# Loads of rotated queries and keys: 32 rows outermost, four parts within

## The chip, the cores and the metric

The program runs on one core of a Trainium2 chip. The metric is the device time of one execution in microseconds (us). The kernel before is given by the median of three runs, and by one further execution that the hardware profiler recorded.

## What is computed

One transformer block on 1024 tokens of width 1024, in float32: a feed-forward block, a token mixer, a second feed-forward block, and a norm. The change lies in the mixer, which has two attentions. Cut to what matters:

```python
# first attention: 8 heads, each with two score maps c = 0, 1 over 64 dimensions
q = apply_rope(q, cos, sin); k = apply_rope(k, cos, sin)
s = einsum('bqhcd,bkhcd->bhcqk', q, k) * HEAD_DIM ** -0.5      # causal
p = softmax(s); a = p[:, :, 0] - lam * p[:, :, 1]
o = einsum('bhqk,bkhe->bqhe', a, v)                            # then a norm per head
# second attention: 16 heads in 2 groups; compressed, selected-block and window branches
qr = apply_rope(q, cos, sin); ks = apply_rope(k_slc, cos, sin); kw = apply_rope(k_win, cos, sin)
o = g0 * o_cmp + g1 * o_slc + g2 * o_win
# mixer
merged = sigmoid(g_a) * (y_da @ w_proj_da) + sigmoid(g_b) * (y_ns @ w_proj_nsa)
x = x + merged @ w_out
```

A rotation pairs dimension d with d + 32, so a head's 64 dimensions are two halves of 32.

## The kernel before, in words

**Layout.** Tokens lie along the free dimension, features on the 128 partitions. Float32 matrices are multiplied as a high and a low part, three products each (`mm3`, lines 52 to 54: `whi`, `wlo` are a weight block's parts). The probabilities and values of the attentions are split into two fp16 halves (`th`, `tl`, lines 974 to 999).

**Rotated queries and keys go through DRAM.** `rope_pair` (from line 612) projects two column blocks of 128, which hold the two halves (32 dimensions each) of four heads or score maps, rotates them on VectorE (lines 625 and 626 read the product out of its bank) and GpSimd, splits them into `rh` and `rl`, and stores those (line 635) into a scratch tensor with dimensions

```python
K.s_q = [dr.tile([3, 2, 4, 32, T], F32, name=f"sq{p}") for p in range(4)]   # part, half, slot, row, token
K.s_k = [dr.tile([2, 2, 4, 32, T], F32, name=f"sk{p}") for p in range(4)]
```

The stores take the 128 rows (slot, row) outermost. The loads read back one slot: `h` (two parts, high and low) and `a` (two halves) give four parts of 32 rows each, which fill 128 partitions. Two neighbouring rows of a part lie 4 KiB apart, two parts 512 KiB. For queries, two such tiles are loaded (`z` = 0: high, low; `z` = 1: low, high), so that two matrix products of 128 rows give the full score.

| Load | Line | Count | Bytes of one, one contiguous run |
|---|---|---|---|
| first attention, queries, `qt<-sq` | 938 | 128 | 128 KB, 1 KB |
| first attention, keys, `kt<-sk` | 1036 | 16 | 512 KB, 4 KB |
| second attention, keys, `kt<-skv` | 1063 | 4 | 512 KB, 4 KB |
| second attention, queries, `qt<-sqn` | 1088 | 64 | 256 KB, 2 KB |

**Who consumes them.** `scores` (line 919) multiplies queries by keys into a PSUM tile `S`; VectorE adds the mask and takes the row's extreme (line 926); ScalarE takes the exponential (line 928); GpSimd and VectorE scale and combine the two maps (lines 960, 962); TensorE transposes blocks of 128 (line 974), ScalarE and VectorE split them into halves (977, 978), and TensorE multiplies them by the values (997 to 999). At the end of half a head the output is squared and summed (lines 1005, 1007, 1014).

**What else runs there.** Between these steps `Filler` deals out projections that do not depend on the attention: queries, keys and values of later heads, gates, and the output projection. They take one PSUM bank (`gm`). Their weight blocks of 512 KB come into `wst` (two buffers, line 1216, before that line 143) and are split by ScalarE and VectorE (lines 1226 and 85, and 89 for the blocks before).

**What sets the order.** The order on each engine is fixed when the program is built. All DMAs are issued by SyncE, one after another in that order; each waits there for what it must follow (a store for its data, a load for its buffer or for the store that it reads). ScalarE and VectorE also work strictly in their order, so a split of weights that waits for its block holds what stands behind it, the exponentials among it. `rh` and `rl` have one buffer each: a new one waits until the stores of the last have landed. The first attention runs from about 970 us to 1460 us of the span, with two heads' projections ahead of it.

Of the kernel before, what the change touches and what calls it, by code (L numbers as in the profile page):

```python
# [7 lines left out]
F32 = mybir.dt.float32  # L8
# [922 lines left out]
def da_queries(K, h, m):  # L931
    nc = K.nc
    qt = []
    p, s0 = h // 2, (h % 2) * 2
    for c in range(2):
        t = K.qp.tile([P, 2, 2 * P], F32R, tag="q", name="qt")
        for z in range(2):
            nc.sync.dma_start(out=t[:, z].bitcast(F32),
                              in_=K.s_q[p][z:z + 2, :, s0 + c, :, m * 256:(m + 1) * 256].rearrange("h a d t -> (h a) d t"))
        qt.append(t)  # L940
    return qt

# [84 lines left out]
def da_load(K, h):  # L1027
    drain([da_load_keys(K, h)])


def da_load_keys(K, h):
    p, s0 = h // 2, (h % 2) * 2
    K.k = []
    for c in range(2):
        t = K.kp.tile([P, T], F32R, tag="k", name="kt")
        K.nc.sync.dma_start(out=t.bitcast(F32), in_=K.s_k[p][:, :, s0 + c].rearrange("h a d t -> (h a) d t"))
        K.k.append(t)
        yield

# [19 lines left out]
def ns_load_key(K, i):  # L1059
    g, br = i // 2, i % 2  # L1060
    pool, tag = [(K.rope, "cR"), (K.rope, "sR"), (K.mp, "m13"), (K.mp, "rh")][i]
    t = pool.tile([P, T], F32R, tag=tag, name="kt")
    order_after(K, K.nc.sync.dma_start(out=t.bitcast(F32), in_=K.s_kv[:, :, br * 2 + g].rearrange("h a d t -> (h a) d t")),
                K.last)
    K.nk[g, br] = t

# [17 lines left out]
def ns_queries(K, hd, H):  # L1084
    qt = []
    for z in range(2):
        t = K.qp[hd % 2].tile([P, TB], F32R, tag=f"q{z}", name="qt")
        K.nc.sync.dma_start(out=t.bitcast(F32), in_=K.s_qns[hd // 4][z:z + 2, :, hd % 4, :, H * TB:(H + 1) * TB]
                            .rearrange("h a d t -> (h a) d t"))
        qt.append(t)  # L1090
    return qt

# [89 lines left out]
def order_after(K, inst, first):  # L1182
    if first is not None:
        K.tc.add_manual_dep(inst.ins, first.ins.name,
                            mybir.DependencyInfo(mybir.DependencyClass.NoSync, mybir.DependencyReason.DATA),
                            reason="order the filler's weights")
# [207 lines left out]
def da_phase(K, cg):  # L1394
    nc = K.nc
    with ExitStack() as ctx:
# [3 lines left out]
        for n, f in enumerate(da_units(K, 0)[:2] + da_units(K, 1)):  # L1400
            if n == 2:
                da_load(K, 0)
            if n == 3:
                da_load_values(K, 0)
            if n == 4:
                q0 = da_queries(K, 0, 0)
                da_split_values(K, 0, K.gm, "gm")
            drain([f()])
# [28 lines left out]
        for p in range(4):  # L1437
            fill.pace(3 * (p + 1) if p < 2 else 6 + ng * (p - 1), PACE_DA)
            for h in (2 * p, 2 * p + 1):
                if h:  # L1440
                    da_load(K, h)
                if h in (4, 6):
                    da_load_values(K, h)
                for m in range(4):
                    qt = q0 if h + m == 0 else da_queries(K, h, m)
                    if h == 4:
                        ns_load_key(K, m)
                    if m == 2 and h + 1 in (1, 2, 3, 5, 7):
                        da_load_values(K, h + 1)
                    res = da_scores(K, h, m, qt, fill.step)  # L1450
                    if pend:
                        finish(*pend)
                    if m == 0 and h in (4, 6):
                        da_split_values(K, h, K.tr, "tr")
                    if m == 3 and h + 1 in (1, 2, 3, 5, 7):
                        da_split_values(K, h + 1, K.tr, "tr")
                    pend = (h, m, res)
            fill.end()
# [6 lines left out]
def ns_phase(K):  # L1465
    nc = K.nc
    K.low = LOW_NS
    with ExitStack() as ctx:
# [5 lines left out]

        K.qp, K.pcp = [pool("nq0")], [pool("npc0")]
        q0 = ns_queries(K, 0, 0)
        pc0 = ns_compressed(K, 0, 0)
        K.qp.append(pool("nq1"))
# [39 lines left out]
        for g in range(2):  # L1518
            for pr in range(4 * g, 4 * g + 4):
                for H in range(2):  # L1520
                    pc = ns_compressed(K, pr, H) if pr + H else pc0
                    y = K.op.tile([P, TB], F32, tag="y", name="y")
                    for par in range(2):
                        hd = pr * 2 + par
                        qt = ns_queries(K, hd, H) if hd + H else q0
                        for m in (2 * H, 2 * H + 1):
                            res = ns_scores(K, hd, m, qt, g, fill.step)
                            if pend:
                                finish(*pend)
                            pend = (hd, m, res, (pc, y), g, par)  # L1530
# [242 lines left out]
```

## Time and profile before

| | before |
|---|---|
| runs: median (lowest, highest) | 2915.92 us (2915.45, 2916.07) |
| profiled execution: its time, its span | 2920.45 us, 2918.7 us |
| TensorE busy | 2795.0 us (96%) |
| VectorE, ScalarE, GpSimd busy | 2001.1, 1392.5, 790.6 us |
| DMA moved, mean rate | 467.74 MB, 160 GB/s |
| share of the 16 DMA engines' span on SyncE's queue | 46.8% |

The profile is of one execution. A row of a timeline has the start in us from the span's start, the duration in us, the engine, the kernel's line, the operation, the tile written, an arrow, the tiles read, and a count where rows were merged; in brackets the time that the engine stood idle before it and what released it. PE is TensorE, DVE VectorE, ACT ScalarE, SPq SyncE's DMA queue; an SPq row's duration is that of issuing, not of the transfer. A row of a stretch has its bounds, its length, the busy time of TensorE, of its weight loads, VectorE, ScalarE and GpSimd with instruction counts in brackets, the granted clock of TensorE as a share of full speed, the mean busy share of the 16 DMA engines, and GB/s. A row of waits has who waited for what, the total in us, how many times, and the longest.

### The profile page before, as it was taken

Reading aid. Unit: us, or ns where it says so; the run is one execution under the profiler, and the core shown is the slowest. Engines: PE = TensorE matmul, PEld = TensorE weight load, DVE = VectorE, ACT = ScalarE, POOL = GpSimd, SP = SyncE. Lnnn points to the kernel's source line nnn. Section 1 sums busy time; section 2 is a strip of 40 time slices with the busy share of each in tenths; the row PEclk is TensorE's granted clock in tenths of the full one; section 3 lists DMA queues with packets and bytes.
Section 4 is the critical chain, followed back from the end, with each engine's and each line's share of the span. In section 5 each row is a group of like instructions: output and inputs, shape, how many; then the busy total and the mean of one; then the engine's idle time right before and its main releaser. Section 6 shows DMA issues by size and latency. Waiting matters only on the chain. (4 is left out here: it accounts for less than half of the span.)

```text
span 2918.7 us, 40265 instructions
## 1 busy us (share of the span) xinstructions
PE 2795.0 (96%) x14310; PEld 2038.4 (70%) x14310; DVE 2001.1 (69%) x3414; ACT 1392.5 (48%) x2391; POOL 790.6 (27%) x701
## 2 busy tenths in 40 slices
PE   8999999999999898989999999999999999999998
PEld 6644447887788776777778778888787854444886
DVE  7866866666588466767777777777443976675566
ACT  7533424442333244455566666777433653333443
POOL 3133321000044222322233333333242414223001
PEclk9999999999999999999999999999999999999999
DMA  4355548654456544444332226222843246444854
GB/s 163 120 201 180 174 170 276 217 185 141 137 188 227 192 144 135 167 143 136 131 121 91 84 86 202 88 87 81 305 153 122 80 143 222 158 173 165 296 181 145
DMA packets 208682, 467.74 MB, mean 160 GB/s; under 512 B 20448, under 2 KB 39136, under 8 KB 208480
## 3 DMA queue, kind: packets, MB, share of 16 engines
q1 hardware_dynamic: 208480, 465.16, 46.8%
q8 instruction: 113, 1.85, 0.3%
q14 instruction: 89, 0.73, 0.1%
HBM read 308.32 MB, written 156.76 MB: 159 GB/s over the span
## 5 line engine op out<-in xcount | busy, mean ns | idle before, releaser
L405 PEld LDWEIGHTS <-w 128*128 128x128 f16 x3024 | 297.7, 99 | 385.2 <-issue 35.6
L52 PE MATMUL gm<-hi,whi 128*128 128x512 f32 x880 | 352.9, 401 | 11.6 <-DVE m L626 7.5
L54 PE MATMUL gm<-hi,wlo 128*128 128x512 f32 x880 | 348.2, 397 | 1.4 <-DVE wlo L85 1.4
L53 PE MATMUL gm<-lo,whi 128*128 128x512 f32 x880 | 348.5, 396 | 0.0
L405 PE MATMUL Y<-tf,w 128*128 128x512 f16 x1296 | 298.4, 385 | 21.3 <-DVE u L443 17.1
L919 PE MATMUL S<-kt,qt 128*128 128x320 f32 (+5 forms) x1152 | 271.4, 357 | 17.5 <-ACT Pt L928 7.5
L85 DVE TENSOR_TENSOR wlo<-st,whi 128x1024 fp32r<-128x1024 f32 x154 | 197.4, 1300 | 114.9 <-ACT whi L89 114.0
L978 DVE TENSOR_TENSOR tl<-tr,th 128x512 f16<-128x512 f32 (+2 forms) x384 | 233.8, 618 | 57.2 <-ACT th L977 56.0
L977 ACT ACTIVATE th<-tr 128x512 f16<-128x512 f32 (+2 forms) x384 | 202.4, 542 | 142.1 <-PE tr L974 125.7
L926 DVE CUSTOM_DVE_ANT_0 S<-S,slab 128x896 f32<-128x896 f32 (+7 forms) x320 | 223.9, 709 | 64.4 <-PE S L919 58.6
L89 ACT ACTIVATE whi<-st 128x1024 fp32r<-128x1024 f32 x154 | 160.7, 1057 | 179.4 <-PE acc L54 109.4
L53 PE MATMUL acc<-wlo,whi 128*128 128x512 f32 (+1 forms) x628 | 244.1, 389 | 1.0 <-DVE wlo L85 1.0
L54 PE MATMUL acc<-whi,wlo 128*128 128x512 f32 (+1 forms) x628 | 242.8, 389 | 0.0
L52 PE MATMUL acc<-whi 128*128 128x512 f32 (+1 forms) x628 | 240.4, 387 | 0.0
L919 PEld LDWEIGHTS S<-kt,qt 128*128 128x128 f32 x1152 | 186.2, 195 | 35.1 <-ACT Pt L928 9.8
L1114 POOL TENSOR_SCALAR Ps<-Ps,l 128x384 f32<-128x384 f32 (+7 forms) x128 | 101.9, 796 | 377.9 <-DVE l L1112 279.3
L52 PEld LDWEIGHTS gm<-hi,whi 128*128 128x128 f32 x880 | 167.4, 190 | 45.1 <-DVE m L626 10.0
L405 PE MATMUL X<-h,w 128*128 128x512 f16 x864 | 195.3, 379 | 1.0 <-ACT s L415 1.0
L54 PEld LDWEIGHTS gm<-hi,wlo 128*128 128x128 f32 x880 | 166.9, 190 | 37.0 <-DVE wlo L85 2.0
L53 PEld LDWEIGHTS gm<-lo,whi 128*128 128x128 f32 x880 | 167.4, 190 | 30.6 <-issue 0.4
L85 DVE TENSOR_TENSOR wlo<-wst,whi 128x1024 fp32r<-128x1024 f32 x103 | 141.9, 1380 | 62.5 <-ACT whi L89 40.4
L521 POOL TENSOR_TENSOR u<-u,u 128x512 f32<-128x512 f32 x36 | 52.7, 1463 | 349.1 <-DVE sa L102 164.3
(340 smaller groups left out, 6063.2 us busy)
## 6 DMA issues: line engine op xcount, KB each, us to landing
wst<-in_win_dram SPq DMA_DIRECT2D x55, 512.0 KB
sw<-w2s SPq DMA_DIRECT2D x44, 512.0 KB
st<-sw SPq DMA_DIRECT2D x88, 256.0 KB
st<-saT SPq DMA_DIRECT2D x88, 256.0 KB
a<-in_f1w_dram SPq DMA_DIRECT2D x36, 512.0 KB
a<-in_f2w_dram SPq DMA_DIRECT2D x36, 512.0 KB
st<-saB SPq DMA_DIRECT2D x66, 256.0 KB
qt<-sq SPq DMA_DIRECT2D x128, 128.0 KB
```

What stands on the lines that cost most here:

```text
L52: first = nc.tensor.matmul(out, lhsT=w[0][:, wk], rhs=x[0], start=start, stop=False, skip_group_check=skip)
L53: nc.tensor.matmul(out, lhsT=w[0][:, wk], rhs=x[1], start=False, stop=False, skip_group_check=skip)
L54: nc.tensor.matmul(out, lhsT=w[1][:, wk], rhs=x[0], start=False, stop=stop, skip_group_check=skip)
L85: return nc.vector.tensor_tensor(out=lo, in0=src, in1=hi.bitcast(F32), op=ALU.subtract)
L89: nc.scalar.activation(out=hi, in_=src, func=AF.Copy)
L405: K.mark = nc.tensor.matmul(o, lhsT=w[:, a, m * h + k], rhs=x[k][:, b], start=start and k == 0 and i == 0, stop=k == h - 1 and i == 2, ski ...
L521: nc.gpsimd.tensor_tensor(out=a, in0=a, in1=b, op=ALU.mult)
L919: K.last = nc.tensor.matmul(S[:, o:o + n], lhsT=q, rhs=k[:, k0 + c:k0 + c + n], start=i == 0, stop=i == 1)
L926: nc.vector.tensor_tensor_reduce(out=sv, in0=sv, in1=mv, scale=-0.125, scalar=BIG, op0=ALU.add, op1=ALU.min, accum_out=nm)
L977: nc.scalar.activation(out=hi[:, 0:n], in_=tr[:, 0:n], func=AF.Copy)
L978: nc.vector.tensor_tensor(out=lo[:, 0:n], in0=tr[:, 0:n], in1=hi[:, 0:n], op=ALU.subtract)
L1114: nc.gpsimd.tensor_scalar(out=p[:, 0:n], in0=p[:, 0:n], scalar1=l[:, c:c + 1], scalar2=P_NS, op0=ALU.mult, op1=ALU.mult)
```

## The change

Each of the four loads keeps its tile, its bytes, its line and its place in the order; every engine's instructions stand in the same order in both builds. Only the order in which the DRAM side is walked differs: before, the outermost dimension is the four parts (4 steps of 512 KiB), then 32 rows of 4 KiB, then the tokens; after it, 32 rows outermost, then the four parts. The SBUF side is 128 partitions in both.

```diff
@@ da_queries
-                              in_=K.s_q[p][z:z + 2, :, s0 + c, :, m * 256:(m + 1) * 256].rearrange("h a d t -> (h a) d t"))
+                              in_=K.s_q[p][z:z + 2, :, s0 + c, :, m * 256:(m + 1) * 256].rearrange("h a d t -> d (h a) t"))
@@ da_load_keys
-        K.nc.sync.dma_start(out=t.bitcast(F32), in_=K.s_k[p][:, :, s0 + c].rearrange("h a d t -> (h a) d t"))
+        K.nc.sync.dma_start(out=t.bitcast(F32), in_=K.s_k[p][:, :, s0 + c].rearrange("h a d t -> d (h a) t"))
@@ ns_load_key
-    order_after(K, K.nc.sync.dma_start(out=t.bitcast(F32), in_=K.s_kv[:, :, br * 2 + g].rearrange("h a d t -> (h a) d t")),
+    order_after(K, K.nc.sync.dma_start(out=t.bitcast(F32), in_=K.s_kv[:, :, br * 2 + g].rearrange("h a d t -> d (h a) t")),
@@ ns_queries
-                            .rearrange("h a d t -> (h a) d t"))
+                            .rearrange("h a d t -> d (h a) t"))
```

So partition 32 j + r held row r of part j, and partition 4 r + j holds it now, in queries and keys alike.

## The prediction

> **What bounds the kernel now.** I read the page first, then the stretches by stage, then TensorE's timeline for its gaps, and last what stood on SyncE's queue and the DMA engines before each gap. The page has TensorE as the bound:
>
> ```profile
> PE   8999999999999898989999999999999999999998
> ```
>
> Each digit is a fortieth of the span in tenths; the 8s after the start lie in the first attention. The stretches (length, each engine's busy time, then TensorE's granted clock, the DMA engines' mean busy share, GB/s) say how much is lost there:
>
> ```profile
> 940.00:1460.00 520.00, 471.85 (x2413) 378.36 (x2412) 341.65 (x722) 244.73 (x485) 136.35 (x130) 0.95 0.44 150
> 1460.00:2050.00 590.00, 573.91 (x3865) 470.52 (x3864) 455.04 (x1177) 398.78 (x913) 197.03 (x267) 1.00 0.31 104
> ```
>
> First attention: 48.2 us idle of 520 at a mean clock of 0.95. Second attention: 16.1 us of 590 at 1.00. Both use the loads that the change rewrites, so the gain has to come from the first. Its gaps on TensorE (start, duration, line, in brackets the idle time before it and its releaser) that have a DMA behind them are these:
>
> ```profile
> 977.12 0.45 PE L919 MATMUL S<-kt,qt 128*128 128x128 f32 x1 [4.38 <-issue]
> 982.21 1.19 PE L919 MATMUL S<-kt,qt 128*128 128x128 f32 x4 [3.58 <-DMA kt<-sk]
> 1007.58 0.50 PE L52 MATMUL gm<-hi,whi 128*128 128x512 f32 x1 [0.93 <-ACT whi L89]
> 1009.19 0.50 PE L54 MATMUL gm<-hi,wlo 128*128 128x512 f32 x1 [0.76 <-DVE wlo L85]
> 1112.88 0.32 PE L997 MATMUL o<-th,vt 128*128 128x256 f16 x1 [2.58 <-ACT th L977]
> 1152.00 0.37 PE L997 MATMUL o<-th,vt 128*128 128x256 f16 x1 [3.99 <-ACT th L977]
> 1154.14 0.80 PE L919 MATMUL S<-kt,qt 128*128 128x256 f32 x2 [0.92 <-ACT Pt L928]
> 1280.17 0.79 PE L919 MATMUL S<-kt,qt 128*128 128x256 f32 x2 [4.19 <-ACT Pt L928]
> ```
>
> Only the second names a DMA. The others name ScalarE, which was itself held, in order, by a store that had not landed or a weight block that had not come:
>
> ```profile
> 1005.52 1.06 ACT L89 ACTIVATE rh<-m 128x1024 fp32r<-128x1024 f32 x1 [8.14 <-DMA sq<-rh]
> 1106.73 1.06 ACT L1226 ACTIVATE whi<-wst 128x1024 fp32r<-128x1024 f32 x1 [3.16 <-DMA wst<-in_win_dram]
> 1150.41 1.06 ACT L1226 ACTIVATE whi<-wst 128x1024 fp32r<-128x1024 f32 x1 [10.45 <-DMA wst<-in_win_dram]
> 1278.20 1.06 ACT L1226 ACTIVATE whi<-wst 128x1024 fp32r<-128x1024 f32 x1 [5.88 <-DMA wst<-in_win_dram]
> ```
>
> Why they are late is seen in stretches of 1 us, whose last two numbers are the busy share of the 16 DMA engines and GB/s:
>
> ```profile
> 957.00:958.00 1.00, 1.00 (x6) 0.84 (x5) 1.00 (x1) 0.00 (x0) 0.00 (x0) 1.00 0.28 98
> 963.00:964.00 1.00, 1.00 (x6) 0.81 (x6) 0.98 (x2) 0.00 (x0) 0.14 (x1) 1.00 1.05 398
> 966.00:967.00 1.00, 1.00 (x6) 0.84 (x5) 0.00 (x0) 0.03 (x1) 0.39 (x1) 1.00 0.25 98
> 970.00:971.00 1.00, 1.00 (x7) 0.81 (x6) 1.00 (x2) 0.00 (x0) 0.00 (x0) 1.00 0.21 53
> 979.00:980.00 1.00, 0.00 (x0) 0.00 (x0) 0.02 (x1) 0.46 (x2) 0.00 (x0) 0.50 0.25 102
> 999.00:1000.00 1.00, 1.00 (x6) 0.84 (x5) 1.00 (x2) 0.00 (x0) 0.00 (x0) 1.00 1.08 399
> ```
>
> With queries (957) or keys (979) alone under way, the share stands on a plateau of 0.25 at about 100 GB/s: four of sixteen engines, at full rate each. When the rotated queries are stored, 128 rows outermost (999), it is 1.08 at 399. So these loads, four parts outermost, run on four engines, and every other transfer, whose pieces lie on all sixteen, is finished only when its pieces on those four are. SyncE's queue (start, time to issue) shows the same from its side:
>
> ```profile
> 968.18 4.24 SPq L1036 DMA_DIRECT2D kt<-sk  x4
> 972.51 8.96 SPq L635 DMA_DIRECT2D sq<-rh  x2
> 997.41 0.90 SPq L635 DMA_DIRECT2D sq<-rh  x2
> 1096.73 0.98 SPq L1216 DMA_DIRECT2D wst<-in_win_dram  x1
> 1132.80 1.09 SPq L938 DMA_DIRECT2D qt<-sq  x2
> 1136.31 4.12 SPq L1216 DMA_DIRECT2D wst<-in_win_dram  x1
> 1260.69 1.07 SPq L938 DMA_DIRECT2D qt<-sq  x2
> 1264.57 3.81 SPq L1216 DMA_DIRECT2D wst<-in_win_dram  x1
> ```
>
> Two stores issue in 0.90 us when nothing is in the way, and in 8.96 us behind four key loads. The weight block issued at 1136.31 is read at 1150.41, 14.1 us later.
>
> **The change part by part.** No instruction is added, removed or moved on any engine: all four edits are one edit to 212 loads (128 and 64 of queries, 16 and 4 of keys), and their bytes and contiguous runs (1, 2 or 4 KB) stay. The score products sum the same 128 rows in another order, at no cost, since queries and keys are permuted alike. What changes is how many engines carry a load and which addresses they read together.
>
> *The rate of a new load.* The trace has no load with 32 rows outermost. The upper bound is 399 GB/s (999 above). The lower one is the nearest load that takes rows from two places per step, the blocks for compression, 64 rows outermost with two parts within, 256 KiB apart:
>
> ```profile
> 697.73 1.23 SPq L788 DMA_DIRECT2D bt<-sraw  x2
> 702.00:703.00 1.00, 1.00 (x6) 0.81 (x6) 0.96 (x5) 0.00 (x0) 0.00 (x0) 1.00 1.04 225
> ```
>
> All engines are busy, but at 225 GB/s. The new loads read four parts 512 KiB apart. I take 399, since the stores of 999 write two parts 512 KiB apart at that rate into all 128 partitions, as the new loads fill all 128, while the 225 row fills 64; but every step below is worked at both.
>
> Two rules of the Trainium skill read the 225 row differently. "DMA: Bandwidth & Descriptors", section "Latency and other measured facts", gives 207 GB/s for row pitches of 512 KiB, which speaks against this change; by it the new loads are the row's kind. "SBUF — State Buffer", section "Door 1: The DMA port swizzle", says that 64 partitions reach only half of the ports; by it the row's slowness is its own. The row agrees with either, and no row here separates them; since the sum holds at 225, it would be the same by both.
>
> *Place 1, the start (977 and 982).* TensorE stood from 972.7 for the first two key tiles. Their loads left at 968.18, after SyncE had waited for the stores of the keys:
>
> ```profile
> SPq L1036 <- DMA sk<-rl: 8.7, 1, 8.7
> ```
>
> At 963 all engines worked, at 966 only the four laggards. Without the laggards the stores are in by about 964.5 at the latest. The first bytes follow an issue by about 1.8 us (968.18, and 970 in the rows), and two tiles, 1.05 MB, take 2.6 to 4.7 us: landed by 969 to 971, before 972.7. 4.38 + 3.58 = 7.96 us go.
>
> *Place 2 (1007 and 1009).* The split of weights stood behind `rh`, which waited 8.14 us for stores that had needed 8.96 us to issue. With no backlog they leave 8 us earlier; 0.93 + 0.76 = 1.69 us go.
>
> *Place 3 (1112).* The weight block left at 1096.73 and came at 1106.73. Alone, behind two query loads, it takes 1.8 us and 0.79 MB at 225 to 399 GB/s, 2.0 to 3.5 us: in by 1102, before ScalarE is free at 1103.57. 2.58 us go.
>
> *Place 4 (1152 and 1154).* From 1132.80 on, four query loads, a key load and the block, 1.57 MB, take 1.8 + 3.9 to 7.0 us: in between 1138.5 and 1141.6, where ScalarE was free at 1139.96 and TensorE stood from 1148.0. At the worst 1.6 us of the 10.45 stay, and TensorE sees none of it. 3.99 + 0.92 = 4.91 us go.
>
> *Place 5 (1280).* The same six transfers from 1260.69: in by 1269.5 at the latest, ScalarE free at 1272.3. 4.19 us go.
>
> Together 21.3 us of standing. After four of these places the granted clock is at the lower of its two levels for a while:
>
> ```profile
> 977.00:987.00 10.00, 6.31 (x18) 5.05 (x19) 2.72 (x10) 1.48 (x6) 0.37 (x1) 0.52 0.46 182
> 1113.00:1117.00 4.00, 3.73 (x19) 3.37 (x18) 1.70 (x4) 2.09 (x4) 2.07 (x3) 0.58 0.06 23
> 1152.00:1158.00 6.00, 5.08 (x20) 3.73 (x20) 4.57 (x14) 4.12 (x13) 3.04 (x4) 0.55 0.26 99
> 1280.00:1284.00 4.00, 3.83 (x11) 3.16 (x12) 2.96 (x10) 3.39 (x12) 1.75 (x3) 0.57 0.26 103
> ```
>
> Busy time times what the clock lacks: 6.31 x 0.48 + 3.73 x 0.42 + 5.08 x 0.45 + 3.83 x 0.43 = 8.5 us. If the gaps close, that is not lost. Sum: 29.9 us. In the second attention I count nothing: 16.1 us of idle, in gaps under 1.6 us, none put down to a load.
>
> The profiled execution took 2920.45 us (span 2918.7) and the median of the runs is 2915.92; the sum is some 1% of either, so I take it off the median: 2886.0.
>
> What is late next? Where TensorE no longer waits it meets its own queue; the other idle time of the stretch, 48.2 - 21.3 = 26.9 us, and its clock loss stay in the forecast. Part of it may go too, since ScalarE and VectorE are held less: a half, 13 us, with 3 us of clock, sets the low side at 2870. Its high side is 2893, with 7 us kept by waits of the kind next described.
>
> **The rivals.** *Another lateness comes up.* In the later heads TensorE already waits for ScalarE at the end of a head's half, with no DMA in it:
>
> ```profile
> 1300.70 2.08 PE L1014 MATMUL tot<-sq,ones 128*128 128x512 f32 x2 [2.17 <-ACT sq L1007]
> 1301.00:1308.00 7.00, 6.20 (x23) 4.30 (x22) 2.14 (x4) 3.05 (x5) 0.59 (x1) 0.53 0.54 166
> ```
>
> One costs 2.17 us and 6.20 x 0.47 = 2.9 us of clock, 5.1. If the standing had covered three such waits in the early heads, 15.3 us come back: 2901.3. For it: ScalarE's chain is what TensorE waits for at places 3 to 5. Against: ScalarE was itself held there.
>
> *The loads are not spread.* If 32 rows outermost still go to four engines, nothing moves: 2916. Against it: 64 rows outermost gave a share of 1.04. The Trainium skill, "DMA: Bandwidth & Descriptors", section "Why a DMA increments its semaphore by 16 and not by 1", has the engine count as the largest up to 16 that divides both sides' slowest dimension; by it 4 becomes 16, and the plateau of 0.25 agrees with its 4.
>
> *The loads become slower than on four engines.* Sixteen engines reading four parts 512 KiB apart in step could fall below the 100 GB/s of the plateau; that is the point from which the change costs. At 50 GB/s the backlog doubles, and with it the 29.9 us: 2945.8, now with all sixteen engines held. For it: 399 falls to 225 in the row with two parts. Against: 225 is over twice the plateau.
>
> **How the numbers follow.** Forecast 0.64; another lateness 0.21; not spread 0.09; slower loads 0.06. The range holds the first two: 2868 (the low side and 2 us for the unknown) to 2905 (2901.3 and 4). Measurement can tell about 0.2%, 6 us. Faster 0.85, same 0.09, slower 0.06.
>
> **What would show it.** In the changed profile: no plateau of 0.25 while queries or keys load; key loads under way at 200 GB/s or more; no SyncE issue of several us behind them; the eight gaps gone from TensorE and the clock at 1.00 after them; idle time in the first attention near 27 us; the second attention as it was. The prediction is wrong if the plateau stays, if the share is 1.0 at about 100 GB/s or less, or if new gaps named ScalarE take the old ones' places.

## The result and the profile after

| | before | after |
|---|---|---|
| median (lowest, highest), 4 runs each | 2915.99 us (2915.45, 2924.96) | 2888.11 us (2887.27, 2890.81) |
| ratio, 95% interval | | 0.9899 (0.9879 to 0.9919) |
| profiled execution, its span | 2920.45, 2918.7 us | 2888.1, 2886.3 us |

The change saves 27.9 us by the medians, 29.5 us (23.6 to 35.3) by the ratio; the forecast was 29.9 us and a time of 2886.0. The two profiled executions differ by 32.4 us, since the one of before ran 4.5 us above its median; what is read from the two profiles below adds up to 32.4.

The stretches of the kernel after, with the same bounds as those of before (length, busy times, then granted clock, DMA share, GB/s):

```profile
940.00:1460.00 520.00, 489.01 (x2577) 393.97 (x2576) 368.17 (x772) 262.70 (x521) 147.44 (x139) 0.98 0.47 158
1460.00:2050.00 590.00, 573.81 (x3885) 470.35 (x3884) 444.63 (x1146) 394.01 (x898) 189.54 (x258) 1.00 0.34 117
```

Idle time of TensorE in the first stretch is 31.0 us where it was 48.2, and the clock 0.98 where it was 0.95; the second stretch is as it was. (As the kernel is faster, some 30 us of the second attention now lie in the first stretch; up to 1430 us, the work of the old stretch, 28.3 us are idle, and the prediction looked for some 27.) All of TensorE's gaps over 0.75 us from 960 to 1280 us, in its timeline:

```profile
1064.64 0.80 PE L52 MATMUL gm<-hi,whi 128*128 128x512 f32 x1 [2.16 <-DVE m L626]
1092.20 0.50 PE L52 MATMUL gm<-hi,whi 128*128 128x512 f32 x1 [1.12 <-DVE m L626]
1099.95 0.27 PE L997 MATMUL o<-th,vt 128*128 128x256 f16 x1 [0.79 <-ACT th L977]
1161.54 0.27 PE L998 MATMUL o<-tl,vt 128*128 128x256 f16 x1 [1.45 <-DVE tl L978]
1193.46 0.50 PE L52 MATMUL gm<-hi,whi 128*128 128x512 f32 x1 [1.46 <-DVE m L626]
1214.21 0.50 PE L52 MATMUL gm<-hi,whi 128*128 128x512 f32 x1 [1.38 <-DVE m L626]
1273.72 1.12 PE L1014 MATMUL tot<-sq,ones 128*128 128x512 f32 x2 [2.17 <-ACT sq L1007]
```

The gaps at the start, before the products with the values at place 4 and before the scores at place 5 are not there; place 3 keeps 0.79 us of 2.58. What is left was there before and has no DMA behind it. On ScalarE one wait of over 1 us for a weight block is left in the first attention, at place 4, and TensorE does not stand for it:

```profile
1129.38 1.06 ACT L1226 ACTIVATE whi<-wst 128x1024 fp32r<-128x1024 f32 x1 [3.17 <-DMA wst<-in_win_dram]
```

SyncE's queue at the same places as before (start, time to issue) is not held any more: two stores behind four key loads issue in 0.88 us, where it took 8.96.

```profile
962.91 2.46 SPq L1036 DMA_DIRECT2D kt<-sk  x4
968.19 0.88 SPq L635 DMA_DIRECT2D sq<-rh  x2
1119.04 1.16 SPq L938 DMA_DIRECT2D qt<-sq  x2
1122.54 0.59 SPq L1216 DMA_DIRECT2D wst<-in_win_dram  x1
1123.18 0.51 SPq L1036 DMA_DIRECT2D kt<-sk  x1
1125.14 0.33 SPq L667 DMA_DIRECT2D sv<-vr  x1
1125.56 0.63 SPq L1216 DMA_DIRECT2D wst<-in_win_dram  x1
```

Stretches of the kernel after: the key loads under way (965), the 10 us in which TensorE had stood at place 1, and the clock after places 4 and 5:

```profile
965.00:966.00 1.00, 1.00 (x7) 0.81 (x5) 0.00 (x0) 0.00 (x0) 1.00 (x2) 1.00 0.98 393
973.00:983.00 10.00, 10.00 (x48) 8.38 (x47) 7.22 (x15) 3.50 (x8) 3.91 (x3) 1.00 0.86 295
1129.00:1135.00 6.00, 6.00 (x36) 5.05 (x35) 5.07 (x13) 5.08 (x14) 1.28 (x1) 1.00 0.30 102
1251.00:1257.00 6.00, 6.00 (x36) 4.96 (x35) 5.00 (x18) 5.44 (x16) 1.70 (x3) 1.00 0.54 146
```

Keys move at 393 GB/s with all engines busy, TensorE is busy throughout, and the clock stays at 1.00. That sixteen engines now carry a load is also in the counts of DMA packets, before and after:

```profile
DMA packets 208682, 467.74 MB, mean 160 GB/s; under 512 B 20448, under 2 KB 39136, under 8 KB 208480
```

```profile
DMA packets 211226, 467.75 MB, mean 162 GB/s; under 512 B 22992, under 2 KB 41680, under 8 KB 211024
```

The bytes are the same and there are 2544 more packets, all of the smallest class: 212 loads times 12. This is what one small packet for each engine and load would give, if a load went from four engines to sixteen. The counts of the experiments below agree with this reading to within 6 packets.

To see where the time came from, the same instruction is looked up in both timelines, before and then after; the difference of the starts is what has been saved up to there.

```profile
1040.76 0.27 PE L997 MATMUL o<-th,vt 128*128 128x256 f16 x1 [0.58 <-ACT th L977]
1182.58 0.27 PE L998 MATMUL o<-tl,vt 128*128 128x256 f16 x1 [1.45 <-DVE tl L978]
1251.83 1.08 PE L919 MATMUL S<-kt,qt 128*128 128x448 f32 x4 [0.58 <-ACT Pt L928]
1403.22 1.13 PE L1014 MATMUL tot<-sq,ones 128*128 128x512 f32 x2 [1.96 <-ACT sq L1007]
```

```profile
1028.24 0.27 PE L997 MATMUL o<-th,vt 128*128 128x256 f16 x1 [0.58 <-ACT th L977]
1161.54 0.27 PE L998 MATMUL o<-tl,vt 128*128 128x256 f16 x1 [1.45 <-DVE tl L978]
1230.86 1.07 PE L919 MATMUL S<-kt,qt 128*128 128x448 f32 x4 [0.60 <-ACT Pt L928]
1372.41 1.13 PE L1014 MATMUL tot<-sq,ones 128*128 128x512 f32 x2 [1.96 <-ACT sq L1007]
```

With the row at 1300.70, shown with the prediction, which is at 1273.72 now:

| part | foretold, gaps + clock | saved there |
|---|---|---|
| places 1 and 2 | 9.65 + 3.03 = 12.7 us | 1040.76 - 1028.24 = 12.5 us |
| places 3 and 4 | 7.49 + 3.86 = 11.4 us | 21.0 - 12.5 = 8.5 us |
| place 5 | 4.19 + 1.65 = 5.8 us | 27.0 - 21.0 = 6.0 us |
| later heads | 0 | 30.8 - 27.0 = 3.8 us |
| after that | 0 | 32.4 - 30.8 = 1.6 us |

At 930 us, ahead of all places, the kernel after is 0.7 us behind, so places 1 and 2 brought 13.2 us rather than 12.5.

### The profile page after: what moved, and what is told of

It is laid out like the page before. It is cut to its first block, busy times and chain, and to the rows that moved or that the text cites. A ratio compares the mean times of both kernels' runs of the same rounds, so it can differ in the third digit from the quotient of the medians.

```text
span 2886.3 us, 40265 instructions
## 1 busy us (share of the span) xinstructions
PE 2784.0 (96%) x14310; PEld 2032.7 (70%) x14310; DVE 2006.2 (70%) x3414; ACT 1392.8 (48%) x2391; POOL 796.1 (28%) x701
```

## The experiments

Theory: four engines carried all of a load, and what lay behind it on those four came late; sixteen engines remove that. Rivals: the order of rows and addresses does it; the order of instructions does it; only one of the two kinds of load matters; the second attention has a share in it. Every ratio below is to the kernel before.

In the first five kernels a helper stands in the place of the four loads. What is called the control is the kernel with two loads of 16 rows.

**The old row order on sixteen engines.**

```diff
+def load_rows(K, t, src):
+    return [K.nc.sync.dma_start(out=t[(2 * h + a) * 32:(2 * h + a + 1) * 32].bitcast(F32), in_=src[h, a])
+            for h in range(2) for a in range(2)]
```

> Rows lie on the partitions as before the change, and only the spreading is new: each of the four parts is a load of its own, 32 partitions with 32 rows outermost. If the gain comes from the number of DMA engines that carry a load, this takes about the changed kernel's time, 2880 to 2900 us (the instructions' order differs somewhat, as there are more loads), with no plateau of 0.25 in the DMA share. If it comes from the new order of rows or addresses, it stays at 2916 us.

Measured: 2886.85 us, ratio 0.9904 (0.9889 to 0.9919). The whole gain comes with rows and addresses as they were, so the row order is not needed for it. As there are more loads, the instructions stand in another order too, and the kernel with four engines in the order of the control, below, shows that this can bring a part of the time; what this kernel shows by itself is that TensorE no longer stands at places 1, 2, 4 and 5 with the old rows on sixteen engines.

**Two loads of 16 rows, and of 25 and 7.**

```diff
+def load_rows(K, t, src):
+    return [K.nc.sync.dma_start(out=t[4 * r.start:4 * r.stop].bitcast(F32), in_=src[:, :, r].rearrange("h a d t -> d (h a) t"))
+            for r in (slice(0, 16), slice(16, 32))]
```

The second has `(slice(0, 25), slice(25, 32))` in the last line.

> The changed kernel's row order, each load cut into two of 16 rows outermost (64 partitions each). A control for the doubled number of loads. Both theories: 2880 to 2900 us.

> As the control with two loads, but cut into 25 and 7 rows, so that 25 rows can only be shared by five engines. Instructions stand in the same order as in the control. If the number of engines decides, the fullest engines carry 24 of 128 rows where the control's carry 8 and the kernel before had 32: (24 - 8) / (32 - 8), two thirds, of the gain of 28 us is lost, 10 to 25 us over the control, with a DMA share near 0.3 while loads run alone. If the order of rows or addresses decides, it takes the control's time within 6 us.

Measured: 2883.53 us, ratio 0.9892 (0.9875 to 0.9909), and 2885.58 us, 0.9901 (0.9886 to 0.9916). There is no difference that can be told, where 10 to 25 us were expected. Yet the loads did run on few engines. The page of the second:

```profile
DMA packets 210380, 467.77 MB, mean 162 GB/s; under 512 B 22144, under 2 KB 40832, under 8 KB 210176
```

1698 more than before the change, and 212 x (5 + 7 - 4) = 1696. A stretch in which queries and stores are under way (the first key load is issued at 963.90), and TensorE's gap at place 1:

```profile
962.00:965.00 3.00, 3.00 (x15) 2.49 (x14) 1.29 (x2) 0.00 (x0) 1.61 (x2) 1.00 0.35 125
```

```profile
975.46 0.70 PE L919 MATMUL S<-kt,qt 128*128 128x128 f32 x4 [2.56 <-DMA kt<-sk]
```

Share 0.35, and the second key tile comes 2.56 us late: with the new row order on few engines the lateness of place 1 is back, but small. So the loss does not go with the rows on the fullest engine.

The control is not a control at full rate, though. While its key loads are under way:

```profile
966.00:968.00 2.00, 2.00 (x11) 1.65 (x10) 0.00 (x0) 0.96 (x1) 1.01 (x1) 1.00 0.97 242
```

All engines are busy at 242 GB/s, where the changed kernel's keys move at 393: each load of the control fills 64 partitions and not 128. From 967 to 971 the kernel with 25 and 7 rows moves its keys at 148 GB/s and a share of 0.38, so in the keys' rate the two kernels are nearer than their rows on the fullest engine say. That 242 GB/s cost nothing that can be told bears out the prediction, which worked its sum at both ends of 225 to 399 GB/s.

**Four engines in the order of the control.** This tells apart what 24 and 32 of 128 rows do, in one order of instructions.

```diff
-    return [K.nc.sync.dma_start(out=t[4 * r.start:4 * r.stop].bitcast(F32), in_=src[:, :, r].rearrange("h a d t -> d (h a) t"))
+    return [K.nc.sync.dma_start(out=t[4 * r.start:4 * r.stop].bitcast(F32), in_=src[:, :, r].rearrange("h a d t -> (h a) d t"))
```

> The control with two loads of 16 rows, in the same order of instructions, but each walked with the four parts outermost: four engines carry 32 of 128 rows each, as before the change. The 25 and 7 rows had 24 of 128 on five engines and cost nothing. If the number of engines decides and the wait begins between 24 and 32 rows, this takes 20 to 40 us more than the control: 2903 to 2924 us. If the gain of these kernels came from the order of their instructions, it takes the control's time within 6 us.

Measured: 2900.49 us, ratio 0.9936 (0.9917 to 0.9955). That is 0.0044 above the control's, 13 us: the engines cost time here too, with nothing else changed, but less than the 20 us that the theory gave at least, and less than the 29 us of the kernel before. Its timeline says where (its lines are up to 4 higher):

```profile
975.91 0.30 PE L919 MATMUL S<-kt,qt 128*128 128x128 f32 x1 [1.79 <-issue]
980.89 1.19 PE L919 MATMUL S<-kt,qt 128*128 128x128 f32 x4 [4.04 <-DMA kt<-sk]
```

Place 1 is back. Places 3 to 5 are not (a new stand of 2.03 and 1.45 us comes at 1295, where ScalarE had waited 6.74 us for another store), and on ScalarE the weight block of place 4 waits for TensorE to free its buffer, not for a DMA:

```profile
1139.02 1.06 ACT L1229 ACTIVATE whi<-wst 128x1024 fp32r<-128x1024 f32 x1 [1.74 <-PE gm L53]
```

SyncE's queue shows why. The doubled loads changed the order in which the program was built, and the blocks stand ahead of key loads that stood ahead of them before:

```profile
1132.98 0.45 SPq L1219 DMA_DIRECT2D wst<-in_win_dram  x1
1133.48 1.65 SPq L932 DMA_DIRECT2D qt<-sq  x3
1135.17 0.51 SPq L932 DMA_DIRECT2D kt<-sk  x1
1136.21 0.32 SPq L667 DMA_DIRECT2D sv<-vr  x1
1136.63 0.38 SPq L1219 DMA_DIRECT2D wst<-in_win_dram  x1
1137.06 2.21 SPq L932 DMA_DIRECT2D kt<-sk  x3
```

So with four engines the order of instructions seems to decide about places 3 to 5: beside the kernel before, this one is 18.7 us faster on as many engines, with each load cut into two. With sixteen the order makes no difference that can be told. In the change itself the order is the same on both sides.

**Two engines.**

```diff
+def load_rows(K, t, src):
+    return [K.nc.sync.dma_start(out=t[h * 64:(h + 1) * 64].bitcast(F32), in_=src[h]) for h in range(2)]
```

> The old row order, each load cut into two whose outermost dimension is 2: two engines carry all of it, at an estimated 50 GB/s. This is the price of the third rival of the prediction, which doubled the 29.9 us: 2945.8 us. If the number of engines decides, 2935 to 2990 us and a plateau of 0.125 in the DMA share. If the order of rows decides, 2916 us.

Measured: 3144.12 us, ratio 1.0783 (1.0765 to 1.0801), far over either figure. A stretch of 2 us, the waits in the first attention, and the issues of its queries (shortest, median and longest in ns, first and last start):

```profile
982.00:984.00 2.00, 0.00 (x0) 0.00 (x0) 0.00 (x0) 0.00 (x0) 0.00 (x0) 0.50 0.13 53
```

```profile
PE S L919 <- DMA qt<-sq: 71.0, 22, 12.0
ACT whi L1228 <- DMA wst<-in_win_dram: 70.5, 5, 26.9
```

```profile
L932 SPq DMA_DIRECT2D qt<-sq x256: 484/1286/10236, 942.1 to 1665.0; - x128
```

The plateau is 0.13, as expected. An estimate says why it costs so much. The loads of the first attention's stretch are 128 queries, 16 keys of the first attention and four of the second, 27.3 MB: 68 us at 400 GB/s, 273 us at 100, 546 us at 50. What else moved in that stretch before was 150 GB/s x 520 us less 27.3 MB, 50.7 MB or 127 us at the rate of sixteen engines. On the fullest engines that makes 400 us with four engines, where 500 us lie between the first query and the last (943.3 to 1443.2), and 673 with two: more than that, so the backlog cannot drain, and the time between them grows to the 723 us above.

**Keys alone, queries alone, one attention alone.** The loads of before and the changed ones stand side by side, with the instructions in the order of before; only the lines named are changed.

```diff
 keys of the first attention only: line 1036       queries of the first attention only: line 938
 first attention only: lines 938 and 1036          second attention only: lines 1063 and 1088
-"h a d t -> (h a) d t"
+"h a d t -> d (h a) t"
```

> Only the keys of the first attention take 32 rows outermost; its queries stay as before, so its scores multiply unlike rows. By the prediction's places: the key tiles still leave at about 968 us, behind stores held by queries on four engines, but land 5 us sooner (places 1 and 2, 10 to 12 us), place 3 stays, places 4 and 5 close, since of six transfers ahead of the weight block only the queries are slow (13 us): 23 to 26 us under the kernel before, 2889 to 2894 us. Rival, the two kinds add up in the share of their bytes (10.5 of 26.6 MB in the first attention): 2904 us.

Measured: 2894.21 us, ratio 0.9909 (0.9891 to 0.9927): 26.5 us of the 29. (The shares in this expectation count the second attention's four key tiles with the keys; those of the first attention are 8.4 MB, its queries 16.8.)

> Only the queries of the first attention take 32 rows outermost; its keys stay as before, so its scores multiply unlike rows. The key tiles leave at about 963 us and land on four engines at about 975: 5 of the 8 us of place 1 go, place 2 closes, places 3 to 5 close: 20 to 27 us under the kernel before, 2889 to 2896 us. Rival, in the share of the bytes: 2898 us.

Measured: 2903.32 us, ratio 0.9937 (0.9917 to 0.9957): 18.4 us, under what the theory gave. The shares of the bytes have it the wrong way round: the keys are half the bytes of the queries and bring more, though the two intervals overlap a little. In its timeline the gaps at places 1, 4 and 5 are smaller than before, and still there:

```profile
975.54 0.70 PE L919 MATMUL S<-kt,qt 128*128 128x128 f32 x4 [2.40 <-DMA kt<-sk]
1138.96 0.27 PE L997 MATMUL o<-th,vt 128*128 128x256 f16 x1 [1.33 <-ACT th L977]
1141.11 0.80 PE L919 MATMUL S<-kt,qt 128*128 128x256 f32 x2 [1.44 <-ACT Pt L928]
1265.17 0.51 PE L919 MATMUL S<-kt,qt 128*128 128x256 f32 x2 [1.88 <-ACT Pt L928]
```

At the plateau's 100 GB/s a key load on four engines takes an estimated 5 us, and one is issued shortly before and one right after each of these weight blocks; that this is why the gaps stay was not tried. The two parts do not add up: 26.5 and 18.4 us alone, 29 together. Either brings more than half of the whole; that what then stays of the backlog lies largely within the time that the instructions have to spare is the reading that fits.

> Only the first attention's loads are changed (queries and keys), the second's stay as before. The prediction counts nothing in the second attention: 2886 to 2890 us. Rival, part of the gain comes from there: over 2892 us.

Measured: 2891.11 us, ratio 0.9899 (0.9884 to 0.9915): all of the gain.

> Only the second attention's loads (its queries and its four key tiles) are changed. The prediction counts nothing there, but the four key tiles are loaded during the first attention, one ahead of place 5: 2911 to 2917 us. Rival, spreading helps wherever it is: 2905 us or less.

Measured: 2912.78 us, ratio 0.9991 (0.9981 to 1.0001): none that can be told.

**The slow row of the prediction.** The loads of the compression blocks, 225 GB/s, with the distance of their two parts changed:

```diff
-        K.s_raw = [dr.tile([P, T], F32, name=f"sraw{h}") for h in range(2)]
+        K.s_raw = [dr.tile([P, T + 64], F32, name=f"sraw{h}") for h in range(2)]
```

> The changed kernel with the rows of the raw projections' scratch padded from 4096 to 4352 bytes, so that the two parts of a compression block's load lie 272 KiB apart in place of 256. Nothing else is changed. If the distance of a power of two made those loads slow (225 GB/s), they run near 390 GB/s now; if it was that they fill 64 partitions, they stay at 200 to 235 GB/s. No change of the whole time that can be told.

Measured: 2883.74 us in one run, and while those loads are under way:

```profile
700.00:701.00 1.00, 1.00 (x6) 0.81 (x5) 0.89 (x5) 0.00 (x0) 0.00 (x0) 1.00 1.06 233
```

As slow as before: the distance is not the cause. That they fill 64 partitions is what remains of the two readings, and the control above speaks for it: keys with parts 512 KiB apart move at 242 GB/s in loads of 64 partitions and at 393 in loads of 128.

**The control again, beside the changed kernel.**

> The control with two loads of 16 rows again, beside the changed kernel, to see whether it beats it: its order puts weight blocks ahead of key tiles on SyncE's queue. By the gaps of its profile (27.0 us where the changed kernel has 32.2) it would be about 3 us faster; if that is within the spread of runs, no difference.

> The changed kernel again, on the same chip as the control with two loads: 2886 to 2891 us.

Measured: 2883.41 us, ratio 0.9889 (0.9873 to 0.9904), and 2887.72 us, 0.9899 (0.9882 to 0.9916). The intervals overlap, and 4 us of 2888 are under the 0.2% that can be told: no version here beats the changed kernel clearly.

## Why the prediction was right

**The engines.** Right: the plateau of 0.25 is gone, a load has twelve small packets more, and the old row order on sixteen engines brings the same gain. The rivals of loads not spread and of loads slower than before fall.

**The rate.** The bound of 399 GB/s held (393 with keys under way), with four parts 512 KiB apart. The reason given for it does not hold, though: the row at 999 is of stores, which read SBUF and write DRAM, and so says nothing of loads into 128 partitions; the control's 242 GB/s and the changed kernel's 393 do. The Trainium skill's "DMA: Bandwidth & Descriptors", section "Latency and other measured facts", has 207 GB/s for a row pitch of 512 KiB, measured on tiles of 128 rows of 16 KiB. These loads walk 32 rows 4 KiB apart and at each row only four parts 512 KiB apart, and do not show that loss: for this shape the measurement decides. The padded scratch speaks against a cause of that kind in the 225 row too. The Trainium skill's "SBUF — State Buffer", section "Door 1: The DMA port swizzle", has 64 partitions reach half of the ports; the 225, 233 and 242 GB/s of loads into 64 partitions against the 393 into 128 agree in kind, at somewhat more than half.

**Places 1, 2 and 5.** Right in mechanism and size: 12.5 us (13.2 with the late start) against 12.7, and 6.0 against 5.8. The key loads leave at 962.91, and TensorE does not stand.

**Places 3 and 4.** The mechanism held and the term was 2.9 us too large. The working at place 4 failed, though it cost nothing. It let only what was issued ahead of the weight block share the engines with it: it put the block in at 8.8 us or less from the first of the six issues, and ScalarE's wait at 1.6 us or less. The first of them leaves at 1119.04 now, so 1127.8 at the latest; ScalarE starts at 1129.38, after a wait of 3.17. A second key load, a store of values and a second block were issued in between (1123.18 to 1125.56, above). TensorE had the time to spare. What is missing from the term lies elsewhere. Place 3 kept 0.79 us, which no DMA ends. And the granted clock fell to the lower of its two levels where it had not fallen before (the mean of the stretch is 0.57), after a gap that is in both kernels (before, then after):

```profile
1077.00:1081.00 4.00, 3.84 (x17) 3.17 (x18) 3.61 (x9) 2.31 (x6) 0.29 (x1) 1.00 0.28 102
```

```profile
1064.00:1068.00 4.00, 3.36 (x8) 2.72 (x9) 3.77 (x8) 2.65 (x6) 0.07 (x1) 0.57 0.69 248
```

That costs 3.36 x 0.43 = 1.4 us; the last 0.7 us were not traced. The kernel alone does not decide about this fall. There are two profiles of the control, and after this gap the clock is at the lower level in one and at the full one in the other:

```profile
1064.00:1068.00 4.00, 3.43 (x8) 2.70 (x9) 3.71 (x8) 2.65 (x6) 0.01 (x1) 0.59 0.65 176
1064.00:1068.00 4.00, 3.76 (x16) 3.12 (x17) 3.61 (x9) 2.39 (x6) 0.21 (x1) 1.00 0.66 177
```

**What was not counted.** In the later heads 3.8 us came back. Most of it is clock: after the same gap of 2.17 us at the end of a head's half, the clock was 0.53 before, and 6.20 us were worked at it; after, it is 1.00:

```profile
1274.00:1281.00 7.00, 6.10 (x35) 4.63 (x35) 4.42 (x7) 4.27 (x8) 3.18 (x3) 1.00 0.63 225
```

This too differs between executions of one kernel. In the second profile of the changed kernel the same gap of 2.17 us, at 1270.85, is followed by the lower clock, and the later heads bring 1.9 us there in place of 3.8:

```profile
1271.00:1278.00 7.00, 6.20 (x25) 4.70 (x26) 3.66 (x6) 4.12 (x7) 3.05 (x3) 0.59 0.67 225
```

The rival of another lateness had its price from this very row, and the lateness did not come. That the two errors of the sum nearly cancel, -2.9 and +3.8 us, is chance, and so is a part of how near the time came: the profiles differ by 32.4 us where the sum was 29.9, and the medians by 27.9.

**The price of the third rival.** Wrong by far, though the rival did not come: loads on two engines, at 53 GB/s, do not double the loss, they cost 228 us over the kernel before. It was worked out as if waits grew in proportion to the transfers. The kernels with 24, 32 and 64 of 128 rows on the fullest engines show that they do not: nothing that can be told, 13 to 29 us depending on the order, 228 us.

**What stays open.** Why the clock falls after a gap of about 2 us in one execution and not in another of the same kernel was not tried; each such fall costs 1 to 3 us, so a part of the sum by places is not firm to more than that. The wait for weight blocks was seen to depend on SyncE's order, but that order was not changed by itself.

## What to carry to other kernels

Look at the DMA share while one kind of load is alone under way: here a plateau at 4 of 16 engines said that the outermost dimension of the DRAM side was too short, and then everything behind it was late by the backlog of those few engines, under the names of other engines in the list of waits. Working such a gain out place by place, from when the engine that is named was free and when its data came, gave the size to 2 or 3 us here, in part by chance. Adding parts up did not: either half of this change brings more than half of the whole, which fits a cost that starts where the backlog outlasts the time to spare.

## What was not expected of the hardware

- A transfer of another kind pays for the few engines twice: it lands late, and SyncE is held in issuing it (two stores took 8.96 us to issue behind four key loads on four engines, 0.88 us after the change).
- 25 rows outermost run on five engines, by the counts of packets: one small packet for each engine and load.
- Loads into 64 partitions moved at 225 and 233 GB/s with all engines busy, whether their two parts lay 256 or 272 KiB apart, and at 242 GB/s with four parts 512 KiB apart. Loads of the same rows into 128 partitions moved at 393.
- The same gap of 2.2 us was followed by the lower clock in one execution and not in another of the same kernel (0.59 against 1.00).
